# Recurrence of an RWKV-7 layer: pair group by pair group, or all eight pairs of heads chunk by chunk

## The chip, the core and the metric

The program runs on one core of a Trainium2 chip. The metric is device time in microseconds of one launch; lower is better. The core has TensorE (matmuls), VectorE, ScalarE and GpSimd, each with its own queue of instructions, and SyncE, whose queue issues nearly all DMAs. Matmuls read SBUF and write PSUM, which has eight banks of 2 KB a partition.

## The reference

The model is a trunk of two layers for a batch of 1, 1024 tokens and a width of 1024, in float32. Layer 0 mixes tokens with a Hawk block, layer 1 with RWKV-7 time mixing; each layer then has a SwiGLU block and a gated embedding. The part that the change touches is the recurrence of layer 1, over 16 heads of 64:

```python
def rwkv7_scan(r, w, k, v, a_vec, b_vec):
    def step(S, inp):
        r_t, w_t, k_t, v_t, a_t, b_t = inp
        sa = jnp.einsum('bhvk,bhk->bhv', S, a_t)
        S = S * w_t[:, :, None, :] + sa[..., None] * b_t[:, :, None, :] + v_t[..., None] * k_t[:, :, None, :]
        y = jnp.einsum('bhvk,bhk->bhv', S, r_t)
        return S, y
    S0 = jnp.zeros((B, H, N, N), jnp.float32)
    _, y = lax.scan(step, S0, xs)

def rwkv7_time_mix(x, ...):
    ...
    y = rwkv7_scan(rh, heads(decay), kh, vh, -kk, kk * ah)
    mean = jnp.mean(y, axis=-1, keepdims=True)
    var = jnp.mean(jnp.square(y - mean), axis=-1, keepdims=True)
    yn = ((y - mean) * lax.rsqrt(var + RW_GN_EPS)).reshape(B, T, D)
    yn = yn * ln_w + ln_b
    bonus = jnp.sum(rh * kh * r_k, axis=-1, keepdims=True) * vh
    out = (yn + bonus.reshape(B, T, D)) * g
    return out @ w_o, v_first
```

## The kernel before

Activations lie transposed, features on the 128 partitions, in eight tiles of 128 features, and the tokens are handled in two halves of 512 (`t` = 0 and 1). A dense float32 product is made of three fp32r matmuls of 128x128 by 512 (`mm3`, line 246): weights and activations are split into a high and a low part, and the weights are split on the fly by ScalarE and GpSimd (`load_w`, lines 238 and 239). These dense matmuls fill most of TensorE's time.

The recurrence is computed in chunks of 64 tokens, eight to a half. Two heads make a pair and lie on the two halves of the 128 partitions: `E` is partitions 0 to 63, `O` is 64 to 127, and the loops over `HV` visit both. Two pairs make a group; there are eight groups `G`, four for each half of the tokens. Four generators hold the work, written as steps that are divided by `yield`:

- `stage1` (line 990), for each pair: decays, the operands of both sides of the chunk products (`BK`, `ZL`), the scores (`sc`: for each half of the partitions four matmuls of 64 rows, 128 columns and 128 moving columns into one PSUM bank, line 1053, twice for each head), masks, and the transposed `BK` (`bkt`: eight transposes for each head, line 1079).
- `inverse` (line 1098), for each group: the inverse of a triangular 64x64 matrix for each chunk and head, by blocks.
- `stage2` (line 1176), for each group, over its eight chunks: the inputs `zu<-ZL,SV` and half of the outputs `zu<-SV,ZL` (128 rows, 64 columns), a copy `z`, the product with the inverse `zu<-z,V` (64 rows, 64 columns), copies into `SV`, the update of the state `zu<-SV,BKt` (128 rows, 64 columns), and the other half of the outputs `y<-RB,SV` (64 rows, 64 columns). Each burst handles two pairs, so four or eight matmuls. The two halves of the outputs lie in two PSUM tiles and are added by VectorE (line 1233).
- `norm2` (line 1239), for each pair: the norm over a head, the bonus and the gate (`bsum` and `yv`, one fp32 matmul of 512 columns each).

All this is fp32, and such a matmul shows as two records in the trace.

The order on TensorE is written out by hand (`manual_schedule`, line 1269). A planner keeps a clock (`mm`, line 114) that each matmul moves on by its estimated time. After each dense matmul `tick` (line 125) looks whether a generator's next step is due: each `yield` gives a wait in ns, which is multiplied by a slack (3, and 2.5 from line 1362 on), says whether a PSUM bank of the shared ring is needed, and may give a condition, such as `s2[old] >= c4 + 4` in line 1032, by which stage 1 waits until the recurrence of an earlier group has freed its buffers. If it is due, the step's matmuls are put into TensorE's queue at that place, and other engines' instructions go to theirs. `until` (line 148) puts steps into the queue, with no dense work between, until a condition holds; line 1369 does so until all generators have ended, and the tiles behind it reuse their memory. The other engines' queues are ordered by priority (`ahead`, line 107).

## Time and profile before

| what | value |
|---|---|
| median of three runs | 3106.93 us (3098.17 to 3107.34) |
| profiled execution, its own time | 3106.82 us |
| span of the profiled execution | 3105.0 us |
| mean granted TensorE clock | 0.979 |
| TensorE busy | 2958.3 us (95%), 16904 matmul records |
| VectorE busy | 1677.9 us (54%) |
| ScalarE busy | 1438.3 us (46%) |
| GpSimd busy | 1282.7 us (41%) |
| DMA | 336.04 MB, mean 108 GB/s |

The span is the time from the first to the last instruction. PE is TensorE's matmuls, PEld its weight loads, DVE VectorE, ACT ScalarE, POOL GpSimd, and SPq the queue of SyncE. A name such as `zu<-z,V` says that the tile `zu` is written from the tiles `z` and `V`. The granted clock is a share of 2.4 GHz: 1.00 is this, 0.50 is 1.2 GHz.

### The profile page before, as it was taken

What the parts mean: (1) busy time and instruction counts of PE and PEld (TensorE: products, weight loads), DVE (VectorE), ACT (ScalarE), POOL (GpSimd) and SP (SyncE); (2) the same over time, 40 slices, a digit from 0 to 9 for tenths busy, and PEclk for the clock granted to TensorE, in tenths of its full rate; (3) what the DMA queues carried; (4) which work ended last, traced back from release to release, by engine and by line L of the source; (5) the groups of instructions that cost most, each with busy time, mean ns of one, the idle gap of its engine ahead of it and who ended that gap; (6) DMA issues with size and microseconds to landing.
All of it is one profiled execution on the core that took longest, in us unless ns stands there. A gap on an engine that the chain in (4) does not pass through costs nothing. (4 is left out here: it accounts for less than half of the span.)

```text
span 3105.0 us, 45886 instructions
## 1 busy us (share of the span) xinstructions
PE 2958.3 (95%) x16904; PEld 2292.7 (74%) x16904; DVE 1677.9 (54%) x2950; ACT 1438.3 (46%) x2565; POOL 1282.7 (41%) x1080
## 2 busy tenths in 40 slices
PE   5999999999999999999998999999999999999998
PEld 3777778888776777777776667776767777888886
DVE  8756771111563266576678565777866456222145
ACT  5564752222555443444465774454344445322244
POOL 5111134444445444343434344434333355544445
PEclk9999999999998999999999999999999999999999
DMA  3211123333335464333323366423323252333323
GB/s 126 60 36 53 50 79 105 94 94 95 98 126 179 158 190 128 89 111 98 114 91 98 119 204 198 125 85 111 100 88 100 70 185 91 103 95 95 95 81 109
DMA packets 223968, 336.04 MB, mean 108 GB/s; under 512 B 56960, under 2 KB 75136, under 8 KB 223744
## 3 DMA queue, kind: packets, MB, share of 16 engines
q1 hardware_dynamic: 223456, 332.75, 34.9%
q8 instruction: 133, 2.18, 0.3%
q14 instruction: 91, 0.75, 0.1%
q10 hardware_dynamic: 288, 0.37, 0.0%
HBM read 278.24 MB, written 54.79 MB: 107 GB/s over the span
## 5 line engine op out<-in xcount | busy, mean ns | idle before, releaser
L239 POOL TENSOR_TENSOR whl<-raw,whl 128x512 fp32r<-128x512 f32 (+2 forms) x818 | 1061.8, 1303 | 1410.4 <-ACT whl L238 1319.8
L238 ACT CAST whl<-raw 128x512 fp32r<-128x512 f32 (+2 forms) x818 | 482.2, 593 | 851.5 <-PE ops L115 226.2
L115 PE MATMUL ops<-hid,whl 128*128 128x512 f32 x2112 | 523.8, 401 | 13.8 <-DVE hid L290 6.4
L115 PE MATMUL pg<-xn,whl 128*128 128x512 f32 (+1 forms) x2184 | 522.9, 392 | 4.4 <-ACT whl L238 1.9
L115 PEld LDWEIGHTS pg<-xn,whl 128*128 128x128 f32 x2184 | 405.2, 188 | 98.9 <-issue 4.3
L115 PEld LDWEIGHTS ops<-hid,whl 128*128 128x128 f32 x2112 | 392.6, 189 | 113.8 <-DVE hid L290 12.5
L115 PE MATMUL pu<-xn,whl 128*128 128x512 f32 x1584 | 385.9, 396 | 3.1 <-ACT xn L289 1.4
L115 PEld LDWEIGHTS pu<-xn,whl 128*128 128x128 f32 x1584 | 296.0, 189 | 72.0 <-DVE xn L290 2.1
L115 PE MATMUL pps<-mix,whl 128*128 128x512 f32 x1152 | 301.3, 412 | 11.9 <-ACT mix L289 5.1
L390 DVE TENSOR_TENSOR h<-h,ops 128x512 f32<-128x512 f32 x256 | 173.9, 685 | 210.6 <-PE ops L115 208.7
L555 DVE TENSOR_TENSOR sg<-sg,pu 128x512 f32<-128x512 f32 x88 | 60.4, 686 | 396.0 <-PE pu L115 395.4
L115 PEld LDWEIGHTS pps<-mix,whl 128*128 128x128 f32 x1152 | 217.7, 193 | 75.1 <-issue 7.7
L115 PE MATMUL pg<-raw,whl 128*128 128x512 f32 x720 | 198.0, 415 | 0.0
L115 PEld LDWEIGHTS pg<-raw,whl 128*128 128x128 f32 x720 | 134.4, 193 | 34.4 <-issue 3.8
L241 POOL TENSOR_SCALAR whl<-raw 128x512 fp32r<-128x512 f32 (+2 forms) x84 | 58.7, 704 | 217.6 <-PE rps L115 69.7
L115 PE MATMUL pu<-raw,whl 128*128 128x512 f32 x528 | 141.4, 406 | 0.0
L115 PE MATMUL rps<-xn,whl 128*128 128x512 f32 x480 | 123.4, 405 | 16.3 <-ACT xn L289 10.5
L115 PEld LDWEIGHTS rps<-xn,whl 128*128 128x128 f32 x480 | 91.9, 193 | 42.8 <-issue 12.0
L115 PE MATMUL gps<-xn,whl 128*128 128x512 f32 x480 | 117.9, 400 | 0.0
L115 PE MATMUL ops<-m,whl 128*128 128x512 f32 x480 | 114.4, 396 | 0.8 <-ACT m L289 0.8
L115 PEld LDWEIGHTS pu<-raw,whl 128*128 128x128 f32 x528 | 96.1, 188 | 23.8 <-issue 2.6
L115 PEld LDWEIGHTS gps<-xn,whl 128*128 128x128 f32 x480 | 92.3, 192 | 21.4 <-issue 0.5
(277 smaller groups left out, 4027.2 us busy)
## 6 DMA issues: line engine op xcount, KB each, us to landing
raw<-in_ffn_in SPq DMA_DIRECT2D x352, 256.0 KB, 2.6
raw<-in_ffn_out SPq DMA_DIRECT2D x152, 256.0 KB, 2.6
raw<-in_rkv SPq DMA_DIRECT2D x96, 256.0 KB, 3.0
raw<-in_ple_gate SPq DMA_DIRECT2D x64, 256.0 KB, 2.6
raw<-in_w_in SPq DMA_DIRECT2D x48, 256.0 KB, 2.8
h<-h SPq DMA_DIRECT2D x32, 256.0 KB, 3.5
raw<-in_ffn_out SPq DMA_DIRECT2D x48, 128.0 KB, 2.1
raw<-in_w_o SPq DMA_DIRECT2D x24, 256.0 KB, 2.7
```

The lines of the kernel that those rows point to most:

```text
L115: self.nc.tensor.matmul(out, lhsT=lhsT, rhs=rhs, start=start, stop=stop)
L238: nc.scalar.copy(hl[:rows, 0, :w], raw[:rows, :w])
L239: nc.gpsimd.tensor_sub(hl[:rows, 1, :w], raw[:rows, :w], hl[:rows, 0, :w].bitcast(F32))
L241: nc.gpsimd.tensor_scalar(hl[:rows, 0, :w], raw[:rows, :w], 1.0, 0.0, ALU.mult, ALU.add)
L390: nc.vector.tensor_add(hs, hs, ps)
L555: nc.vector.tensor_mul(sg, sg, pu)
```

## The change

- `stage2` runs once for each half of the tokens, chunk by chunk, with all eight pairs in each burst: 16 matmuls for the inputs, 16 for the inverse, 16 for the update, and 32 for the outputs. It begins when all four groups of the half are through stage 1 and the inverse. The outputs' two products go into one PSUM tile, one after the other for each pair and half of the partitions. z, the state and the outputs are handled by instructions over all eight pairs.
- Its operands go through DRAM: stage 1 writes `zl_d` (with the masked scores) and `bk_d`, the inverse writes `inv_d`, and for each chunk the recurrence loads all pairs' operands; the outputs go to `y_d`, from which the norm reads them.
- The scores of a pair's two heads alternate between the row halves, into two banks, in one burst of eight matmuls. The transposes become matmuls against a diagonal (`dg`) that holds the chunk's total decay, and these alternate in the same way, 16 in a burst.
- Stage 1 no longer waits for the recurrence. The shared ring has three PSUM banks instead of two, and a step can ask for two of them. The norm handles the two pairs of a group together.

```diff
-BANKS = 2
+BANKS = 3
...
+C0LAT, ZLAT, ULAT, SLAT = 4000, 900, 900, 3000
...
-        self.vt_d = [[self.dr.tile([64, 2, NC, 64], F32, name=f"vt{j}{t}") for t in range(2)] for j in range(KD)]
+        self.vt_d = [self.dr.tile([64, 2, NC, KD, 64], F32, name=f"vt{t}") for t in range(2)]
...
+        self.zu = pp.tile([128, KD, 64], F32, name="zu")
+        self.yp = pp.tile([128, KD, 64], F32, name="y")
...
+        self.zl_d = [self.dr.tile([128, NC, KD, 320], F32, name=f"zl{t}") for t in range(2)]
+        self.bk_d = [self.dr.tile([128, NC, KD, 128], F32, name=f"bk{t}") for t in range(2)]
+        self.inv_d = [self.dr.tile([128, NC, KD, 64], F32, name=f"inv{t}") for t in range(2)]
+        self.y_d = [self.dr.tile([128, KD, TH], F32, name=f"y{t}") for t in range(2)]
...
+                if g == jj == 0:
+                    PCs[t] = sp.tile([128, NC, KD], F32, tag="PC", name="PC", bufs=2)
+                PC = PCs[t][:, :, j]
                 nc.vector.tensor_copy(PC, Pp[:, :, 64])
-                ZL, RB = [], []
+
+                dg = sp.tile([128, NC, 64], F32, tag="dg", name="dg", bufs=1)
+                nc.gpsimd.tensor_mul(dg, ident.unsqueeze(1).to_broadcast([128, NC, 64]), PC.unsqueeze(2).to_broadcast([128, NC, 64]))
...
-                    yield 0, False, (lambda: old < 0 or s2[old] >= c4 + 4)
...
+                    zr = sp.tile([128, 4, 320], F32, tag="ZL", name="ZL", bufs=2)
+                    zl = zr[:, :, 0:256].rearrange("p c (h k) -> p h c k", h=2)
+                    rb = zr[:, :, 256:320]
...
-                    yield 1500, True, None
-                    for hh, me, ot in HV:
-                        ps = big("sc", 1700).rearrange("p (c s) -> p c s", c=4)
-                        for c in range(4):
-                            self.mm(ps[:, c, :], BK[me, c4 + c, :, :].rearrange("p i s -> p (i s)"), zl[me, hh, c, :])
-                        evac()
-                        m3 = mask.unsqueeze(1).to_broadcast([128, 4, 128])
-                        with self.ahead(AHEAD_S1):
+                    yield 1500, 2, None
+
+                    pss = [big("sc", e).rearrange("p (c s) -> p c s", c=4) for e in (1000, 2000)]
+                    for c in range(4):
+                        for hh, me, ot in HV:
+                            self.mm(pss[hh][:, c, :], BK[me, c4 + c, :, :].rearrange("p i s -> p (i s)"), zl[me, hh, c, :])
+                            if hh:
+                                self.clock -= 200
+                    evac()
+                    evac()
+                    m3 = mask.unsqueeze(1).to_broadcast([128, 4, 128])
+                    with self.ahead(AHEAD_S1):
+                        for hh, me, ot in HV:
+                            ps = pss[hh]
                             nc.vector.tensor_mul(AB[me, cs, :], ps[me, :, 0:64], m3[me, :, 0:64])
                             nc.vector.tensor_mul(rb[me], ps[me, :, 64:128], m3[me, :, 64:128])
                             nc.vector.tensor_mul(zl[ot, hh], ps[ot], m3[ot])
-                        if hh == 0:
-                            yield 0, True, None
-                yield 0, True, (lambda: (G == 0 or inv[G - 1] >= 1) and (old < 0 or s2[old] == NC))
+                    nc.sync.dma_start(self.zl_d[t][:, cs, j, :], zr)
+                yield 0, 2, (lambda: (G == 0 or inv[G - 1] >= 1))
...
-                for hh, me, ot in HV:
-                    ps = c3(big("bkt", 800))
-                    for c in range(NC):
-                        nc.tensor.transpose(ps[:, c, :], BK[me, c, :, :].rearrange("p i s -> p (i s)"), ident[me])
...
+                pss = [c3(big("bkt", e)) for e in (500, 900)]
+                for c in range(NC):
+                    for hh, me, ot in HV:
+                        self.mm(pss[hh][:, c, :], BK[me, c, :, :].rearrange("p i s -> p (i s)"), dg[me, c, :])
+                        self.clock -= 77
+                evac()
+                evac()
+                with self.ahead(AHEAD_S1):
+                    for hh in range(2):
+                        nc.scalar.copy(BKt[:, :, hh, :], pss[hh])
+                nc.sync.dma_start(self.bk_d[t][:, :, j, :], BKt.rearrange("p c h k -> p c (h k)"))
...
-                yield 0, False, (lambda: G == 0 or s2[G - 1] == NC)
...
+                nc.sync.dma_start(self.inv_d[G // 4][:, :, 2 * (G % 4) : 2 * (G % 4) + 2, :], Vt)
...
         def stage2():
             ahead = lambda: self.ahead(AHEAD_S2)
+            def state():
+                return sp.tile([128, 2, KD, 64], F32, tag="SV", name="SV", bufs=2)
+            def load(t, c, SV):
+                ZL = sp.tile([128, KD, 320], F32, tag="ZC", name="ZC", bufs=2)
+                V = sp.tile([128, KD, 64], F32, tag="VC", name="VC", bufs=2)
+                for hh, me, ot in HV:
+                    nc.sync.dma_start(SV[ot, hh], self.vt_d[t][:, hh, c])
+                nc.sync.dma_start(ZL, self.zl_d[t][:, c])
+                nc.sync.dma_start(V, self.inv_d[t][:, c])
+                return ZL, V, SV
+            def load_u(t, c):
+                SU = sp.tile([128, 2, KD, 64], F32, tag="SU", name="SU", bufs=1)
+                BKc = sp.tile([128, KD, 128], F32, tag="BC", name="BC", bufs=1)
+                for hh, me, ot in HV:
+                    nc.sync.dma_start(SU[ot, hh], self.vt_d[t][:, hh, c])
+                nc.sync.dma_start(BKc, self.bk_d[t][:, c])
+                return SU, BKc
+            SV = state()
+            for hh, me, ot in HV:
+                nc.gpsimd.memset(SV[me, hh], 0.0)
+            for t in range(2):
+                yield 0, False, (lambda: inv[4 * t + 3] == 3 and s1[4 * t + 3] == 22 and all(have("v", j, t)() for j in range(KD)))
+                PC = PCs[t]
+                nxt = load(t, 0, SV)
+                yield C0LAT, False, None
                 for c in range(NC):
+                    ZL, V, SV = nxt
+                    SU, BKc = load_u(t, c)
                     upd = not (t == 1 and c == NC - 1)
+                    ps, yp = self.zu, self.yp
+                    z = sp.tile([128, KD, 64], F32, tag="z", name="z", bufs=1)
+                    at = self.clock
+                    for j in range(KD):
                         for hh, me, ot in HV:
+                            self.mm(ps[me, j, :], ZL[:, j, hh * 128 : hh * 128 + 64], SV[:, hh, j, :])
+                    self.clock = at + 650
+                    with ahead():
+                        nc.scalar.copy(z, ps)
+                        if upd:
+                            ss = sp.tile([128, KD, 64], F32, tag="ss", name="ss", bufs=1)
+                            for hh, me, ot in HV:
+                                nc.vector.tensor_mul(ss[me], SV[me, hh], PC[me, c, :].unsqueeze(2).to_broadcast([64, KD, 64]))
+                            SVn = state()
+                        if c < NC - 1:
+                            nxt = load(t, c + 1, SVn)
+                    yield ZLAT, False, None
+                    at = self.clock
+                    for j in range(KD):
                         for hh, me, ot in HV:
+                            self.mm(ps[me, j, :], V[me, j, :], z[me, j, :])
+                    self.clock = at + 600
+                    with ahead():
+                        nc.scalar.copy(SU[E, 0], ps[E])
+                        nc.vector.tensor_copy(SU[O, 1], ps[O])
+                    yield ULAT, False, None
+                    at = self.clock
+                    if upd:
+                        for j in range(KD):
+                            for hh, me, ot in HV:
+                                self.mm(ps[me, j, :], BKc[:, j, hh * 64 : hh * 64 + 64], SU[:, hh, j, :])
                         with ahead():
+                            for hh, me, ot in HV:
+                                nc.vector.tensor_add(SVn[me, hh], ps[me], ss[me])
+                    for j in range(KD):
                         for hh, me, ot in HV:
+                            self.mm(yp[me, j, :], SV[:, hh, j, :], ZL[:, j, hh * 128 + 64 : hh * 128 + 128], True, False)
+                            self.mm(yp[me, j, :], SU[me, hh, j, :], ZL[me, j, 256:320], False, True)
+                    self.clock = at + 2000
+                    if c % 2 == 0:
+                        ys = sp.tile([128, KD, 2, 64], F32, tag="yc", name="yc", bufs=1)
+                    with ahead():
+                        nc.scalar.copy(ys[:, :, c % 2, :], yp)
+                    if c % 2:
+                        nc.sync.dma_start(self.y_d[t][:, :, c * 64 - 64 : c * 64 + 64], ys.rearrange("p j c k -> p j (c k)"))
                     if upd:
+                        SV = SVn
+                    s2[t] = c + 1
+                    yield SLAT, False, None
...
         def norm2():
...
+                yield Y1, 2, None
...
+                yield 2400, 2, None
...
```

## Rows read from the trace of the kernel before

**Rows 1.** The page's engine line: busy us, share of the span, instructions.
```profile
PE 2958.3 (95%) x16904; PEld 2292.7 (74%) x16904; DVE 1677.9 (54%) x2950; ACT 1438.3 (46%) x2565; POOL 1282.7 (41%) x1080
```
**Rows 2.** Windows: stretch, its length, busy us (records) by engine, clock, DMA share, GB/s.
```profile
500.00:800.00 300.00, 298.29 (x1292) 241.96 (x1292) 65.85 (x81) 90.50 (x150) 140.00 (x108) 1.00 0.31 94
1125.00:1715.00 590.00, 565.53 (x4178) 430.16 (x4177) 399.82 (x837) 274.24 (x554) 249.64 (x206) 0.98 0.37 109
1950.00:2530.00 580.00, 558.05 (x4527) 420.44 (x4527) 388.07 (x839) 254.73 (x537) 232.16 (x179) 0.98 0.35 103
```
**Rows 3.** TensorE's timeline, one chunk step: start, length, operation, tiles, records.
```profile
1277.99 0.34 PE L115 MATMUL zu<-SV,ZL 128*64 128x64 f32 x4
...
1278.61 1.88 PE L115 MATMUL ops<-hid,whl 128*128 128x512 f32 x7
1280.42 0.45 PE L115 MATMUL zu<-z,V 64*64 64x64 f32 x8
1280.80 2.34 PE L115 MATMUL ops<-hid,whl 128*128 128x512 f32 x9
1283.07 0.45 PE L115 MATMUL zu<-SV,BKt 128*64 128x64 f32 x8
1283.45 0.45 PE L115 MATMUL y<-RB,SV 64*64 64x64 f32 x8
1283.83 2.59 PE L115 MATMUL ops<-hid,whl 128*128 128x512 f32 x10
1286.34 0.34 PE L115 MATMUL zu<-SV,ZL 128*64 128x64 f32 x4
```
**Rows 4.** TensorE's timeline at a burst of scores.
```profile
1238.04 1.16 PE L115 MATMUL sc<-ZL,BK 64*128 64x128 f32 x8
1239.13 1.66 PE L115 MATMUL pu<-xn,whl 128*128 128x512 f32 x6
1240.72 1.16 PE L115 MATMUL sc<-ZL,BK 64*128 64x128 f32 x8
```
**Rows 5.** TensorE's timeline at a burst of transposes.
```profile
1264.73 0.70 PE L1079 MATMUL bkt<-cst,BK 64*128 64x64 f32 x8
1265.36 3.00 PE L115 MATMUL ops<-hid,whl 128*128 128x512 f32 x12
```
**Rows 6.** The tile of the scores: records, ns min/median/max, first and last start.
```profile
L115 PE MATMUL sc<-ZL,BK x512: 271/272/580, 1132.4 to 2358.8; 64*128 64x128 f32 x171
```
**Rows 7.** TensorE's timeline at the lora matmuls (128 and 64 rows in turn).
```profile
955.45 4.24 PE L115 MATMUL lx<-lora,whl 128*128 128x512 f32 x10
...
965.98 13.06 PE L115 MATMUL lx<-lora,whl 128*128 128x512 f32 x18 [3.61 <-DVE y L766]
```
**Rows 8.** Windows around them and at a short stretch of lower clock.
```profile
955.40:961.30 5.90, 5.42 (x14) 2.22 (x13) 4.03 (x7) 2.74 (x4) 4.15 (x4) 1.00 0.51 162
961.30:981.80 20.50, 16.89 (x27) 7.69 (x27) 7.28 (x10) 17.29 (x31) 8.09 (x7) 0.50 0.59 218
1582.50:1585.90 3.40, 3.40 (x9) 2.73 (x9) 2.04 (x6) 1.48 (x5) 0.00 (x0) 0.50 0.30 77
```
**Rows 9.** Groups of ScalarE: count, busy us, mean ns, idle before, releasers.
```profile
L1203 ACT ACTIVATE ss<-SV,PC 64x64 f32<-64x64 f32 x240 | 82.8, 345 | 51.5 <-DVE SV L1220 41.4 <-DMA SV<-st 4.7 <-DMA st<-ss 1.6
```
**Rows 10.** Waits of TensorE, 1125 to 2530 us: total, times, longest us.
```profile
PE zu L115 <- DVE z L1199: 4.7, 4, 2.0
```
**Rows 11.** Waits of SyncE's queue in the same stretch.
```profile
SPq L227 <- POOL whl L239: 834.9, 332, 10.4
```
**Rows 12.** TensorE's timeline at the end of the scan.
```profile
2503.51 1.02 PE L115 MATMUL yv<-v,cst 128*128 128x512 f32 x2
...
2524.32 5.76 PE L115 MATMUL pg<-raw,whl 128*128 128x512 f32 x24
```

More of the change, by code (lines that the diff above doesn't have):

```diff
@@ L122, in ready @@
         lat, bank, cond = st.need
-        return (cond is None or cond()) and max(lat, self.bank_free[self.bank_n % BANKS] if bank else 0.0)
+        return (cond is None or cond()) and max([lat] + [self.bank_free[(self.bank_n + i) % BANKS] for i in range(int(bank))])
     def tick(self, wait=False):
@@ L959, in t3 @@
         def t3(nm):
-            return sp.tile([128, TH], F32, tag="t3", name=nm, bufs=2)
+            return sp.tile([128, TH], F32, tag="t3", name=nm, bufs=4)
         def ld(nm, j, t, tt=tt):
@@ L1170, in inverse @@
                     for p0 in (0, 64):
[L1171 to L1172 removed]
+                        nc.scalar.copy(V[p0 : p0 + 32, :, :, 32:64], ps[p0 : p0 + 32].rearrange("p (j c) k -> p j c k", j=2))
+                nc.sync.dma_start(self.inv_d[G // 4][:, :, 2 * (G % 4) : 2 * (G % 4) + 2, :], Vt)
                 yield 1000, False, None
@@ L1177, in stage2 @@
             ahead = lambda: self.ahead(AHEAD_S2)
-            for G in range(NG):
-                t, g = G // 4, G % 4
-                pairs = 2 * g, 2 * g + 1
-                yield 0, False, (lambda: inv[G] == 3 and s1[G] == 22 and (G == 0 or n2[G - 1]))
-                ys = [sp.tile([128, TH], F32, tag="ys", name="ys", bufs=2) for j in pairs]
+            def state():
[8 more added lines that the diff above has]
+                return ZL, V, SV
@@ L1222, in stage2 @@
-                    for ps, ZL, RB, z, ss, PC, BKt, SV, V, yp in T:
-                        for hh, me, ot in HV:
-                            self.mm(yp[me, cc, :], SV[me, c, hh, :], RB[me, cc, :])
-                    if upd and c == NC - 1:
-                        for j, x in zip(pairs, T):
-                            nc.sync.dma_start(self.st_d[j], x[4])
-                    if cc == 3:
-                        with ahead():
-                            for jj in range(2):
-                                y = ys[jj][:, (c - 3) * 64 : (c + 1) * 64].rearrange("p (c s) -> p c s", s=64)
-                                nc.scalar.copy(y, yps[:, jj])
-                                nc.vector.tensor_add(y, y, self.zu[jj][:, 3:7])
```

112 lines of the change are left out of this document (30 added, 82 removed).

## The prediction

> **What bounds the kernel now.** The page's engine line comes first: TensorE is busy 95% of the span, no other engine over 54% [rows 1]. So the time is the sum of what is queued on TensorE, plus its waits, plus what a lower clock costs. The windows tell the dense part from the part with the recurrence [rows 2]. From 500 to 800 us there is dense work alone: 1292 matmuls in 298.29 us, 0.231 us each. From 1125 to 1715 and from 1950 to 2530 us the recurrence lies between the dense matmuls; TensorE is idle 24.5 and 22 us there, VectorE is busy 68 and 67%, and the clock is 0.98. An instruction of the recurrence that TensorE no longer runs is therefore saved almost whole, and one that lasts longer there is paid almost whole. VectorE and ScalarE count only where TensorE waits for them.
>
> The timeline of one chunk step is the next view [rows 3]: from 1277.99 to 1286.34 us, 8.35 us, it holds 7 + 9 + 10 = 26 dense matmuls, 6.01 us at 0.231. The recurrence of one pair group and chunk thus costs 2.34 us. There are 64 such steps (8 groups, 8 chunks): 150 us. An fp32 matmul shows as two records. The first burst (8 matmuls, 16 records, one tile shape) reaches the next dense matmul after 0.62 us, the second (4 matmuls) after 0.38 us. Four more matmuls cost 0.24 us, 0.06 each, the two column halves side by side; 0.14 us is left that does not depend on their number. The same 0.38 us stands between the start of the update (128x64) and that of the outputs (64x64), with no dense work and no wait between: a change of tile shape costs 0.14 us there too. The dense runs behind the bursts are longer than their count (7 in 1.81 us instead of 1.62, 9 in 2.27 instead of 2.08, 10 in 2.51 instead of 2.31): 0.20 us more. A burst costs 0.34 us, and 0.06 per matmul.
>
> **The change part by part.** The sum is made against the profiled execution, 3106.82 us (span 3105.0 and 1.8 around it); the median of the runs, 3106.93, is the same.
>
> *Fewer bursts.* Three bursts in each of 64 steps, 192, become three in each of 16 chunks, 48. Inputs (16 matmuls), inverse (16) and update (16) now cost 0.34 + 16 x 0.06 = 1.30 us each, 3.9 us a chunk.
>
> *The outputs of a chunk.* Both products go into one PSUM tile, so for each pair and half the code issues one matmul with 128 rows and then one with 64 rows: 32 in a row whose tile shape changes every time. Before, each kind stood in a group of four. One alone between two changes costs 0.14 us and its own time, from 0.06 us (as beside its partner) to 0.12 (alone): 0.20 to 0.26. The nearest row of such a stream is the lora one, which also changes between 128 and 64 rows each time [rows 7]: 10 matmuls in 4.24 us, 0.42 instead of 0.231, so 0.19 more for each change, which gives 0.06 + 0.19 = 0.25. I take 0.26: 32 x 0.26 = 8.3 us. A chunk then costs 3.9 + 8.3 = 12.2 us, 16 chunks 195 us, against 150 now: **+45 us**. With 0.20 it is 10.3 and 165 us (+15); if the change of shape were free, 32 x 0.06 = 1.9, so 5.8 and 93 us (-57).
>
> This is where the Trainium skill speaks against the change. "TensorEngine Tiling (Array Packing)", Key Properties, says that changing the tiling mode, not only the tile, drains the engine. The trace agrees: 0.14 us at each change [rows 3]. The page gives no duration; read as a drain of the whole array it makes the +45, read tile by tile it makes the first rival.
>
> *The scores.* A burst of four takes 1.09 us to the next dense matmul, and the six dense ones behind it 1.59 instead of 1.39 [rows 4]: 1.29 us. There are 64 (512 records, [rows 6]): 82 us. After, 32 bursts hold eight each, alternating between the row halves in two banks. One matmul with no partner is (1.09 - 0.14)/4 = 0.24 us. Side by side the burst stays at 1.29 us: 41 us in all, **-41**. One after the other it is 0.34 + 8 x 0.24 = 2.24: 72 us, -11. No row shows two row halves at once; the nearest, the column halves of rows 3, do overlap fully, so I take -41.
>
> *The transposes.* A burst of eight takes 0.63 and 0.20 us [rows 5]; 32 make 27 us. They become 16 bursts of 16 fp32 matmuls against a diagonal, their stationary side the same 128 columns as the scores'. At 0.12 each (row halves side by side) a burst is 2.26 us, 36 in all: **+9**. Serial at 0.24 it is 4.2 us: +40. At 0.06, since only 64 columns move: -6. I take +9, as the stationary side equals the scores'.
>
> *The clock.* The lora stream again: 5.9 us after its first matmul, with 0.5 us idle in it, the granted clock falls to 0.50, and it stays there while 18 alternating matmuls run for 13.06 us without a gap, 0.73 each instead of 0.42, 1.7 times as long [rows 7, 8]. The outputs last 8.3 us. If the clock falls 5.9 us into them, the last 2.4 us cost 1.7 more. Then dense work begins at the lower level; the shortest such stretch here is 3.4 us with nine dense matmuls where 14.7 would fit [rows 8], 1.3 us lost. 16 x 3.0 = **+48 us**. Bounds: 0 if it never falls; 90 if it falls halfway and two such stretches follow (16 x (3.0 + 2.6)).
>
> *VectorE, ScalarE.* The small evacuations go: ScalarE's scaling of the state alone is 240 instructions, 82.8 us [rows 9]; 8 wide ones per chunk replace them. Neither engine sets the time, so I cost this at nothing. The waits it could end are few: 4.7 us for z [rows 10]. But stage 1 no longer waits for the recurrence, so its VectorE work moves closer together: VectorE's 400 us in 590 hold four groups and about 130 us of dense work (0.22 of the time [rows 2]), so some 270, under 60 per group without recurrence and output norm. By the waits in the code a group now comes every 70 us or so, with 15 of dense work: VectorE is full there, and TensorE may wait 5 us a group, 40 in all. The other way, half of the 46 us idle could go. I take nothing, from -25 to +40.
>
> *The transfers.* Each chunk now fetches 2.6 MB and stage 1 writes as much, about 80 MB more. All is issued on SP's queue, where weight loads already wait 834.9 us for their buffers, up to 10.4 us at once [rows 11]; behind such a wait stand the new loads. The next chunk's operands are asked for a chunk ahead, over 20 us. The update's come at the start of their own chunk, some 7 us ahead: if one is 4 us late each time, 64 us; I take nothing, since the issue may run ahead of TensorE.
>
> *The end.* The second half's recurrence starts only when all its groups are through stage 1. The last work of the scan stands at 2503.51 us, the dense work that must not start before it at 2524.32 [rows 12]: 21 us of cover. After, from the waits in the code: the first scores still near 1880 us, as r is ready no earlier; a pair's waits are 1 + 4 + 1.5 + 1.5 = 8 us times a slack of 3, with bursts and banks some 36 us, so eight pairs end near 2170; the inverse takes 45; a chunk waits 0.9 + 0.9 + 3 = 4.8 us times 2.5, with its 12.2 some 25, eight of them 200; an output norm waits 7.4 us times 2.5, some 22, four of them 88. That is near 2505, while the dense work moves out with the sum. So nothing; were the waits to be half again as long for the pairs, as waits for banks and VectorE could make them, the end lies some 65 us past the cover.
>
> **Sum**: 3107 + 45 - 41 + 9 + 48 = 3168 us.
>
> **The rivals.**
> 1. *Faster: the changes of shape cost little.* The outputs write one column half after the other; if one half drains while the other runs, a matmul costs 0.13: a chunk 3.9 + 4.2 = 8.1, 130 in all, -20; with -41 and +9 and no fall of the clock, 3055 us. If they are free, -57: 3018. For it: the column halves run side by side in rows 3. Against: the 0.14 us stands at each change there. Without the clock it decides at (150 + 32)/16 = 11.4 us a chunk, less 3.9: 7.5, 0.23 us per output matmul; below that the kernel is faster.
> 2. *The row halves don't overlap*: scores -11 and transposes +40, 61 us more: 3229. For it: no row shows the overlap. Against: the column halves.
> 3. *Late data*: operands behind weight loads (+64), or the scan past its cover (+65): about 3233.
> 4. *The change gives back what it takes*: the clock holds and half of the idle goes: 3107 + 13 - 15 = 3105.
>
> **How the numbers follow.** Forecast 0.48, with its own range from 3091 (0.20 each, clock holds) to 3215 (clock term 90). Rival 1 0.24, rival 2 0.12, rival 3 0.10, rival 4 0.06. About 0.3% (9 us) can be told from no change. Faster: rival 1, 0.03 of the forecast's low end, 0.01 of rival 4: 0.28. Same: 0.03 of the forecast and 0.04 of rival 4: 0.07. Slower: 0.65. The range: rival 1's freer half (0.11) stays out below 3045; rivals 2 and 3 go in up to 3260, which leaves 0.08 above.
>
> **What would show it.** The outputs' run of 64 records per chunk: 8 us long or longer if I am right, 2 us if the changes of shape are free. The score bursts: 1.1 us for 16 records, or 2. The clock row: a fall in most chunks between the first and last of them, or none. Idle of TensorE before the update names a late load; idle before the last output norms, the end. The forecast is wrong if the outputs take under 7 us and the clock stays at 1.00.

## The result and the profile after

The changed kernel takes 3224.57 us (median of four runs, 3217.91 to 3224.96) where the kernel before takes 3102.55 beside it: a ratio of 1.039 [1.036, 1.042], slower. The forecast was 3168 us in a range of 3045 to 3260. The direction and the place of the loss hold. The size does not: +61 us were forecast, and the profiled executions differ by 118 (spans 3222.9 and 3105.0). The measured time also lies above 3215, the upper end of the forecast's own range; it falls into the stated range through the part up to 3260, which was put there for rivals 2 and 3.

The page's engine line of the changed kernel, against [rows 1], shows TensorE 80 us busier although it has nearly the same number of records; VectorE and ScalarE are 60 and 79 us less busy.

```profile
PE 3038.5 (94%) x17160; PEld 2386.2 (74%) x17160; DVE 1618.0 (50%) x2498; ACT 1359.2 (42%) x2213; POOL 1301.1 (40%) x1082
```

The windows, against [rows 2] (the second stretch with the recurrence now ends some 110 us later), show dense work alone unchanged and a clock of 0.94 and 0.89 where it was 0.98.

```profile
500.00:800.00 300.00, 298.29 (x1292) 241.98 (x1291) 65.74 (x80) 90.89 (x150) 139.10 (x108) 1.00 0.31 94
1125.00:1715.00 590.00, 565.08 (x4525) 448.54 (x4524) 338.99 (x614) 222.25 (x383) 226.96 (x180) 0.94 0.50 159
1990.00:2640.00 650.00, 604.89 (x4610) 474.67 (x4608) 338.89 (x594) 215.74 (x366) 227.22 (x178) 0.89 0.46 147
```

TensorE's timeline of one chunk, against [rows 3]. The first three bursts are short: 32 records in 1.08 (1523.50 to 1524.58), 1.08 and 0.98 us. The outputs then run for 9.43 us, a new tile shape every two records: each lone matmul takes 0.26 us (1533.19 to 1533.45), and 0.40 at the end, where the clock has fallen.

```profile
1523.50 1.15 PE L116 MATMUL zu<-SV,ZC 128*64 128x64 f32 x32
1524.58 2.79 PE L116 MATMUL pu<-xn,whl 128*128 128x512 f32 x11
...
1527.75 1.15 PE L116 MATMUL zu<-z,VC 64*64 64x64 f32 x32
1528.83 3.25 PE L116 MATMUL pg<-xn,whl 128*128 128x512 f32 x13
1532.00 1.15 PE L116 MATMUL zu<-SU,BC 128*64 128x64 f32 x32
1532.98 0.28 PE L116 MATMUL y<-ZC,SV 128*64 128x64 f32 x2
1533.19 0.33 PE L116 MATMUL y<-ZC,SU 64*64 64x64 f32 x2
1533.45 0.33 PE L116 MATMUL y<-ZC,SV 128*64 128x64 f32 x2
...
1540.80 0.47 PE L116 MATMUL y<-ZC,SV 128*64 128x64 f32 x2
1541.20 0.47 PE L116 MATMUL y<-ZC,SU 64*64 64x64 f32 x2
...
1542.41 3.88 PE L116 MATMUL pg<-xn,whl 128*128 128x512 f32 x9
```

Windows over the outputs' runs alone (the first, the last, and the sum of all 16) give 155.8 us for them; the clock is below 1.00 in each, 0.64 to 0.87.

```profile
1532.98:1542.41 9.43, 9.43 (x64) 6.82 (x64) 0.00 (x0) 0.00 (x0) 0.00 (x0) 0.82 0.29 86
...
2518.80:2529.89 11.09, 11.09 (x64) 7.94 (x64) 0.00 (x0) 0.00 (x0) 0.00 (x0) 0.64 0.10 25
sum 155.79, PE 155.77 PEld 112.55 DVE 0.68 ACT 0.00 POOL 2.72; mean PE 9.74 PEld 7.03 DVE 0.04 ACT 0.00 POOL 0.17
```

The same windows stretched to 20 us from each run's start hold the dense work behind it as well. Eleven of the 16 read 0.83, four 0.74 and the last 0.66, as in these two; which makes 20 x (11 x 0.17 + 4 x 0.26 + 0.34) x 2 = 130 us at 0.50, 69 of them in the runs and 61 in the dense work behind.

```profile
1532.98:1552.98 20.00, 20.00 (x110) 15.43 (x107) 4.12 (x6) 4.65 (x8) 3.48 (x4) 0.83 0.45 142
...
2518.80:2538.80 20.00, 20.00 (x92) 15.03 (x92) 2.07 (x3) 3.64 (x7) 3.10 (x3) 0.66 0.24 76
```

**A split that serves every run.** I split each span into three: idle time of TensorE (before and between its matmuls), the price of the clock (half of the time that TensorE is busy at 0.50), and the rest, the work at full clock. Before, these are 139, 60 and 2906 us. They are summed over the trace's records; span x (1 - mean clock), which also counts idle time at 0.50, gives 65 for before and 161 instead of 145 for after. The differences against before, in us of the profiled executions:

| kernel | ratio to before | span | work | clock | idle | work by the prediction's terms |
|---|---|---|---|---|---|---|
| the change | 1.039 [1.036, 1.042] | +118 | -4 | +85 | +38 | +13 |
| e1 outputs grouped | 0.996 [0.995, 0.997] | -13 | -88 | +23 | +52 | -89 |
| e2 half the changes of shape | 1.005 [1.004, 1.007] | +13 | -55 | +21 | +46 | -52 |
| e3 outputs in four pieces | 1.047 [1.045, 1.049] | +139 | +16 | +48 | +75 | +29 |
| e4 scores in turn | 1.044 [1.042, 1.045] | +134 | +15 | +81 | +38 | +34 to +49 |
| f3 the scores alone | 1.003 [1.002, 1.004] | +10 | -35 | +15 | +30 | -41 |
| f4 alternating outputs alone | 1.055 [1.052, 1.058] | +174 | +91 | +37 | +45 | +93 |
| n1 before, other order | 1.015 [1.013, 1.017] | +51 | +2 | +19 | +31 | 0 |
| n2 two banks, in turn | 1.002 [1.001, 1.003] | +2 | -17 | -9 | +29 | -11 |
| f1 e1, slower stage 1 | 0.997 [0.996, 0.998] | -20 | -86 | +12 | +53 | -89 |
| f2 e1, operands stored twice | 1.003 [1.002, 1.004] | +2 | -85 | +17 | +70 | -89 |
| f5 e1, norm loads on ScalarE's queue | 1.003 [1.002, 1.005] | +6 | -88 | +25 | +68 | -89 |
| f6 e1, longer bank estimates | 0.998 [0.997, 1.000] | -5 | -83 | +30 | +48 | -89 |

Span, work, clock and idle of a row are of one execution, the ratio of all. For n1 it is the slowest of four (3157.66 us, median 3147.06) and for f1 the fastest of ten (3086.39, median 3094.41), so by the medians n1 is 43 us above the kernel before, not 51, and f1 9 below, not 20.

Two things stand out. In ten of the thirteen the work is within 6 us of the terms. The others are the change, e4 and e3. The change and e4 hold the long alternating runs, and there the split is some 10 us off: at 0.50 an alternating matmul lasts 0.40 us instead of 0.256, 1.57 times as long, not twice, so the half is too much for the 69 us in the runs. The change's own split is then +6 of work and +75 of clock. In e4 the price of the scores was too high as well (below); e3's 13 us less than the terms are not explained. And every kernel that differs from the kernel before has at least 29 us more idle time, n1 too, in which no part of the change is made.

### The profile page after: what moved, and what is told of

Read it like the earlier page. It is cut to its first block, busy times and chain, and to the rows that moved or that the text cites. A ratio compares the mean times of both kernels' runs of the same rounds, so it can differ in the third digit from the quotient of the medians.

```text
span 3222.9 us, 45692 instructions
## 1 busy us (share of the span) xinstructions
PE 3038.5 (94%) x17160; PEld 2386.2 (74%) x17160; DVE 1618.0 (50%) x2498; ACT 1359.2 (42%) x2213; POOL 1301.1 (40%) x1082
## 5 line engine op out<-in xcount | busy, mean ns | idle before, releaser
L116 PE MATMUL ops<-hid,whl 128*128 128x512 f32 x2112 | 513.1, 400 | 19.0 <-ACT hid L290 7.2
L116 PEld LDWEIGHTS ops<-hid,whl 128*128 128x128 f32 x2112 | 400.8, 192 | 119.6 <-DVE hid L291 14.3
L116 PE MATMUL pps<-mix,whl 128*128 128x512 f32 x1152 | 297.6, 412 | 15.2 <-ACT mix L290 4.6
L116 PEld LDWEIGHTS pg<-raw,whl 128*128 128x128 f32 x720 | 145.9, 206 | 39.6 <-ACT whl L239 3.0
L116 PEld LDWEIGHTS pu<-raw,whl 128*128 128x128 f32 x528 | 105.7, 203 | 28.4 <-ACT whl L239 2.2
L291 DVE TENSOR_TENSOR hid<-sg,hid 128x512 fp32r<-128x512 f32 x88 | 86.3, 980 | 49.8 <-ACT hid L290 49.7
```

Source lines behind the costliest of these rows:

```text
L116: self.nc.tensor.matmul(out, lhsT=lhsT, rhs=rhs, start=start, stop=stop)
L291: (nc.gpsimd if pool else nc.vector).tensor_sub(lo, src, hi.bitcast(F32))
```

## The experiments on the outputs

**e1.** All 128-row products of a chunk, then all 64-row ones: one change of shape instead of 32 between the outputs. Each half of the partitions becomes one accumulation group, started once. By the Trainium skill, "PSUM — Partial Sum Buffer", section "The four PSUM rules", a start clears the written marks of the whole bank on all the partition quarters that it writes, so that with a second start the later products would overwrite the first ones instead of being added to them; no run here shows that.

```diff
                     for j in range(KD):
                         for hh, me, ot in HV:
-                            self.mm(yp[me, j, :], SV[:, hh, j, :], ..., True, False)
-                            self.mm(yp[me, j, :], SU[me, hh, j, :], ZL[me, j, 256:320], False, True)
+                            self.mm(yp[me, j, :], SV[:, hh, j, :], ..., j == 0, False)
+                    for j in range(KD):
+                        for hh, me, ot in HV:
+                            self.mm(yp[me, j, :], SU[me, hh, j, :], ZL[me, j, 256:320], False, j == KD - 1)
```

> All 16 output products of 128 rows of a chunk, then all 16 of 64 rows: one change of tile shape instead of 32. Theory (each change costs about 0.14 us and the overlap of the halves, and the long run of changes lowers the clock): a chunk's output run shrinks from 9 to 11 us to about 2.1 (32 x 0.06 + 0.14), 16 x 7.4 = 118 us, the falls of the clock in it go, some 30 us more of dense work at the lower level: 3070 to 3090 us, below the kernel before. Rival (VectorE's lateness in stage 1 and the chunk's loads set the time): within 20 us of the changed kernel, 3205 to 3225.

3093.67 us: 131 us faster than the change, and 0.4% faster than the kernel before; 4 us past the upper end of what was expected. VectorE's and GpSimd's instructions stand in the same order as in the change. The tile's records in e1 (ns min/median/max of one) are as short as in any burst, a chunk's outputs take 2.11 us, and no fall of the clock begins at them:

```profile
L116 PE MATMUL y<-ZC,SV x512: 222/222/270, 1534.0 to 2399.2; 128*64 128x64 f32 x171
L116 PE MATMUL y<-ZC,SU x512: 218/218/267, 1535.0 to 2400.3; 64*64 64x64 f32 x171
```

**e2.** Both heads' 128-row products, then both 64-row ones: 16 pairs instead of 32 lone matmuls.

```diff
                         for hh, me, ot in HV:
                             self.mm(yp[me, j, :], SV[:, hh, j, :], ..., True, False)
+                        for hh, me, ot in HV:
                             self.mm(yp[me, j, :], SU[me, hh, j, :], ZL[me, j, 256:320], False, True)
```

> For each pair both halves' 128-row products, then both 64-row ones: 16 changes of shape a chunk instead of 32, and the halves beside each other. Theory: 2 x 0.14 + 4 x 0.06 = 0.52 us a pair, 4.2 us a chunk instead of 9 to 11, 16 x 5.4 = 86 us; falls of the clock become rare: 3110 to 3140 us. Rival (the cost goes with the number of matmuls, not of changes): no difference, 3215 to 3230.

3120.82 us, as expected. A pair, one head on each column half, takes 0.26 us, as one matmul alone does in the change; a chunk 4.17 us, without a fall. So the price belongs to the change of shape, not to the matmul.

```profile
1534.01 0.29 PE L116 MATMUL y<-ZC,SV 128*64 128x64 f32 x4
1534.22 0.33 PE L116 MATMUL y<-ZC,SU 64*64 64x64 f32 x4
...
1538.17 2.12 PE L116 MATMUL pg<-xn,whl 128*128 128x512 f32 x8
```

**e3.** The same 32 alternating matmuls in four pieces, dense work between them.

```diff
                     for j in range(KD):
+                        if j in (2, 4, 6):
+                            self.clock = at + 600
+                            yield 700, False, None
+                            at = self.clock
...
-                    self.clock = at + 2000
+                    self.clock = at + 600
...
-                    yield SLAT, False, None
+                    yield SLAT - 2100, False, None
```

> The same 32 changes of shape a chunk, but in four pieces with about 2 us of dense work between. Theory with the clock: no piece is long enough for the clock to fall; a piece takes 8 x 0.26 = 2.1 us, three more bursts cost 3 x 0.34 = 1.0 us a chunk (+16), and the 16 falls of 6.8 to 13.7 us go (-50 to -80): 3160 to 3195 us, no fall of the clock at the outputs. Rival (the clock costs nothing here, only the changes of shape): 3230 to 3245.

A piece takes 2.05 us, as expected, and only two falls begin at one. The time is a miss: 3246.14 us. That is next to the rival's band, but not for the rival's reason, as the clock's price fell from +85 to +48 us. The pieces removed most of the outputs' clock price, and the idle time went from +38 to +75. The waits of TensorE in e3 from 1125 to 2700 us (total, times, longest) show loads for which the changed kernel waits 0.5 us in all. The shortened wait in front of the next chunk is the likely reason; no run separates it from the pieces.

```profile
PE zu L116 <- DMA SU<-vt: 14.9, 12, 1.9
PE bsum L116 <- DMA b<-b: 14.8, 4, 6.9
```

**f4.** The kernel before with the outputs' eight matmuls of each step alternating in the last burst. The 128-row products stand behind the write of the solution there and read it in place of the state, so what they compute is another; their number and shapes are the same.

```diff
-                        for hh, me, ot in HV:
-                            self.mm(ps[me, 3 + cc, :], SV[:, c, hh, :], ZL[:, hh, cc, 64:128])
...
                         for hh, me, ot in HV:
+                            self.mm(ps[me, 3 + cc, :], SV[:, c, hh, :], ZL[:, hh, cc, 64:128])
                             self.mm(yp[me, cc, :], SV[me, c, hh, :], RB[me, cc, :])
```

> The kernel before with the other part alone: in each of the 64 chunk steps the four matmuls of 128 rows of the outputs move from the first burst to the last one, where they alternate with the four of 64 rows; 8 matmuls in a row whose tile shape changes each time, some 2 us. Theory A (each lone matmul between two changes of shape costs 0.26 us, whether the clock falls or not): 8 x 0.26 = 2.1 us for the eight, against 8 x 0.06 plus the one change 0.14 = 0.62 that they cost before: +1.46 x 64 = +93 us, near 3197, ratio 1.025 to 1.033, with the granted clock staying up at nearly all of the 64 runs, as they end before 3 us. Theory B (what the changes cost in the changed kernel is mainly the lower clock that follows a long run of them): without a fall of the clock the time rises by 40 us or less, ratio 1.013 or below.

The work is +91 us, and A's +93 holds. But the time is +174, a ratio of 1.055, which neither theory expected. The new place has a wait of its own, of which A took no account (waits of TensorE from 1150 to 2560 us: 33.8 us in 49), and the clock price grew by 37 us: 17 falls begin at or just behind these runs. Runs of 2 us, here with a wait of some 0.6 us in front of each, do not keep the clock up as I expected.

```profile
PE zu L115 <- DVE SV L1218: 33.8, 49, 1.8
```

## The experiments on the scores and the waits

**e4.** The scores of the changed kernel one head after the other, still two banks at once.

```diff
-                    for c in range(4):
-                        for hh, me, ot in HV:
+                    for hh, me, ot in HV:
+                        for c in range(4):
                             self.mm(pss[hh][:, c, :], BK[me, c4 + c, :, :]..., zl[me, hh, c, :])
```

> The scores of one head after those of the other in the same burst, so that neighbouring matmuls lie on the same row half. Theory (row halves run side by side in the changed kernel): the burst of 16 records goes from 0.9 to 1.8 us, 32 x 0.9 = +29 us: 3245 to 3260. Rival (the gain of the score bursts is only their number): 3220 to 3230.

3240.25 us, 16 us slower than the change and between the two bands. In turn a burst lasts 1.64 us to the next dense matmul, where the prediction's price is 2.04 (2.24 less the 0.20 in the dense work behind). Alternating the heads is thus worth 0.55 us a burst, 32 x 0.55 = 18 us, near the 19 by which the work grew. The timeline of e4, and behind it that of the changed kernel, 1.09 us:

```profile
1131.99 1.71 PE L116 MATMUL sc<-ZL,BK 64*128 64x128 f32 x16
1133.63 3.71 PE L116 MATMUL pps<-mix,whl 128*128 128x512 f32 x15
```

```profile
1132.79 1.16 PE L116 MATMUL sc<-ZL,BK 64*128 64x128 f32 x16
1133.88 1.89 PE L116 MATMUL pps<-mix,whl 128*128 128x512 f32 x7
```

**f3.** The kernel before with the row-half scores alone.

```diff
-                    yield 1500, True, None
-                    for hh, me, ot in HV:
-                        ps = big("sc", 1700)...
-                        for c in range(4):
-                            self.mm(ps[:, c, :], BK[me, c4 + c, :, :]..., zl[me, hh, c, :])
+                    yield 1500, 2, None
+                    pss = [big("sc", e)... for e in (1000, 2000)]
+                    for c in range(4):
+                        for hh, me, ot in HV:
+                            self.mm(pss[hh][:, c, :], BK[me, c4 + c, :, :]..., zl[me, hh, c, :])
+                            if hh:
+                                self.clock -= 200
...
```

> The kernel before with one part of the change alone: the scores of the two heads of a pair are issued in turn on the two row halves, into two PSUM banks, in bursts of 16 records; all else stays (chunk steps by pair groups, transposes, outputs in groups of one shape). Theory A (the two halves run side by side, and the saving reaches the end, as my sum has it): a burst of eight lasts about 0.9 us to the next dense matmul, 64 bursts become 32, and the time falls by about 41 us: near 3064, ratio 0.986 to 0.990. Theory B (side by side, but the burst that now needs two banks at once waits for their evacuation, in the middle of the burst, with the lower clock after each such wait): the records stand in pairs as in A, but waits of TensorE of the kind scores on the evacuation of the bank come to 10 us or more, and the time falls by 15 us or less: ratio 0.995 or above.

Most of the 41 us is there (work -35), and none of it arrives: idle +30, clock +15. B's ratio is met (1.003), yet its mechanism is not the one: the waits of the scores for a bank are 5.6 us, and the large ones stand in the norm of the outputs (TensorE's waits from 1150 to 2560 us: total, times, longest).

```profile
PE bsum L115 <- issue: 15.2, 3, 10.1
PE bsum L115 <- DMA b<-b: 10.0, 1, 10.0
...
PE sc L115 <- DVE ZL L1065: 5.6, 4, 2.8
```

**n2.** f3 with the heads in turn (the loops of e4), so that the joint burst and its two banks are new; the planner's clock also counts each matmul in full, without f3's `-= 200`.

> The kernel before with both heads' scores in one burst that needs two banks, as in the change, but one head after the other, not side by side. Work: one fixed cost of 0.34 us less in each of 32 bursts, so -11 us against before. Theory B (the need of two banks at once makes the waits): idle 20 to 35 us more and the clock 5 to 20, as with the scores side by side: ratio 1.004 to 1.014. Theory C (the waits come because side by side the burst ends sooner and its results come faster than VectorE clears them): idle and clock within 10 us of before, ratio 0.993 to 1.000.

Idle +29, as in f3, though the two heads' results now come one after the other: C falls. B's idle time is there, but its clock price is not (-9), and the ratio, 1.002, lies between the bands of the two. The work is -17 where -11 was expected, since a burst in turn is shorter than its price, as in e4.

**n1.** The kernel before with a single estimate changed.

```diff
-                    yield 1500, True, None
+                    yield 2500, True, None
```

> The kernel before, with no part of the change: only the wait that the order by estimates puts before each scores burst is 2500 instead of 1500 ns, so the same instructions stand in another order on TensorE. I split each span into idle time of TensorE, what the lower clock costs (half of the time that TensorE is busy at it) and the rest, its work: the scores alone on the row halves took 35 us of work away and gave back 30 of idle and 15 of clock. Theory A (the order of the kernel before fits its waits closely, and any other order pays for it, whatever was made faster): work within 6 us of before, idle and clock together 20 to 45 us more, ratio 1.006 to 1.014. Theory B (the waits come from what the scores burst newly needs, two banks at once): idle and clock within 10 us, ratio 0.997 to 1.003.

1.0145 [1.0125, 1.0165]: A, a little past the upper end of what A expected. The work is the same within 2 us, idle +31, clock +19, together past the 45 as well, though in the slowest of its four executions. Up to 1715 us it is idle hardly more than the kernel before (26 instead of 24.5 us from 1125 on); 25 of the 31 us stand behind 1950 us. No burst has grown and no second bank is asked for. The longest waits of TensorE from 1125 to 2700 us, of the kernel before, of n1 and of the changed kernel:

```profile
PE bsum L115 <- issue: 8.9, 2, 6.2
PE yv L115 <- ACT v L1252: 5.7, 4, 3.0
```

```profile
PE sc L115 <- DVE ZL L1059: 13.6, 3, 7.2
PE ops L115 <- DVE h L390: 11.4, 5, 5.4
PE nps L115 <- DVE acc L301: 9.6, 4, 4.6
```

```profile
PE sc L116 <- DVE ZL L1072: 16.8, 4, 6.1
PE nps L116 <- DVE acc L302: 9.3, 2, 5.8
PE lx L116 <- DVE o L896: 7.4, 1, 7.4
```

**f6, f5, f1, f2** start from e1 and each take one candidate for its 52 us. f6 sets longer bank estimates, f5 moves the norm's loads from SP's queue to ScalarE's, f1 slows stage 1 in the first half, f2 stores the scores' operands twice.

```diff
-                    pss = [big("sc", e)... for e in (1000, 2000)]
+                    pss = [big("sc", e)... for e in (2500, 3500)]
```

> e1 (outputs grouped by shape), with larger estimates for the evacuation of the two banks of a scores burst (2500 and 3500 ns instead of 1000 and 2000), so that the next burst is set later in the order of TensorE and dense work is put before it. Theory A (a good part of the idle time of TensorE is the scores waiting in the middle of a burst for their second bank): the waits of the scores on VectorE's evacuation fall below 4 us from 10 or more, the idle time of 1158 to 2512 us falls from 112 to under 100 and the time falls by 10 to 20 us: ratio to the kernel before 0.990 to 0.993. Theory B (those waits are only where a delay of VectorE shows first): they move to other lines (inverse, transposes, lora) with the same sum, and the ratio stays within 0.003 of e1's 0.9964.

The scores' waits halve (15.2 to 7.5 us), but the idle time of 1158 to 2512 us goes from 115 to 108 only, the clock gets worse, and the ratio rises to 0.9984 [0.9970, 0.9998]: the waits moved, for example to `ops` (10.5 us at once, behind ScalarE's `on`). A falls. B's ratio is met (0.0020 above e1's), though the waits went to other lines than it named: summed over 1125 to 2700 us, those that end on VectorE fall from 71 to 29 us, and those that end on ScalarE, GpSimd and loads rise from 50 to 87.

```diff
-                    nc.sync.dma_start(ys, self.y_d[t][:, j, :])
+                    nc.scalar.dma_start(ys, self.y_d[t][:, j, :])
...
```

> The changed kernel with its outputs grouped by shape (e1), and in addition the loads of the output norms (y, b, v, g) issued on ScalarE's queue instead of SP's. Theory A (the part of the time that my sum lacks is waits behind SP's queue: the norms' loads and stores stand there in order with those of the dense work): TensorE's idle time between 1707 and 1950 us falls from 39.7 us to 20 or less, and the time falls by 15 to 25 us from e1: ratio to the kernel before 0.988 to 0.992. Theory B (those waits come from the shared transfer engines, or from VectorE's and ScalarE's own order): the idle time stays above 32 us, and the ratio stays between 0.994 and 1.000, or goes up, as ScalarE then stands behind its own loads.

1.003: A falls. Idle of 1707 to 1950 us goes up from 40 to 45 us, and the loads that I moved are now late themselves (waits of TensorE, 1150 to 2560 us):

```profile
PE bsum L116 <- DMA b<-b: 29.3, 6, 10.7
```

```diff
-                yield 4000, False, (lambda: old < 0 or inv[old] >= 2)
+                yield 4000 + 3000 * (t == 0), False, (lambda: old < 0 or inv[old] >= 2)
```

> e1 (the changed kernel with its outputs grouped by shape), with 7000 instead of 4000 ns of waiting between two pairs of heads of stage 1 in the first half. Theory D (stage 1 without its wait on the recurrence runs at the pace of VectorE, and TensorE waits for that): of the 24 us idle and 27 us at the lower clock between 1158 and 1544 us 10 or more of each go, and the ratio to before is 0.990 to 0.994. Rival (any order of this kernel has such waits, they move): idle and clock together within 10 us of e1 or more, ratio 0.995 to 1.000.

Idle of 1158 to 1544 us is 23 us (24 in e1), and the time at the lower clock there falls from 27 to 17 us; but over 1158 to 2512 us the time at the lower clock is the same 126 us, and the ratio lies within e1's interval: the rival. The pace of stage 1 in the first half is not what makes TensorE idle there. The second half was not slowed.

```diff
                     nc.sync.dma_start(self.zl_d[t][:, cs, j, :], zr)
+                    nc.sync.dma_start(self.zl2_d[t][:, cs, j, :], zr)
```

> e1 with each store of the scores' operands (640 KB, 32 times) issued a second time to another place in DRAM: 21 MB more. Theory E (the 80 MB of operands that go through DRAM make part of the waits, by SP's order or by the shared transfer engines): with a quarter more of them idle and clock grow by 10 us or more, ratio 1.000 or above. Rival (the transfers are covered, as my sum has it): within 8 us of e1, ratio 0.994 to 0.999.

1.0033 [1.0022, 1.0044], idle +18 against e1. E's number is met, but not cleanly: TensorE's waits for loads from 1125 to 2700 us are 0.5 us in all (4.8 in e1), so it does not wait for late loads itself; and TensorE's order is the same as e1's, while those of VectorE, ScalarE and SP shift with the 32 added issues, and n1 shows what another order alone can do.

## Why the prediction was right in sign and half in size

- **Fewer bursts and the outputs: right.** 0.26 us for each lone matmul, 32 x 0.26 = 8.3 us a chunk; at full clock the trace has 0.256 (32 in 8.2). e2 and f4 price the same change of shape, and e1 takes it away: 2.11 us, near the 1.9 that I gave to outputs without the changes. The 0.26 measured lies above the point of decision, 0.23 us per matmul, so rival 1 is out.
- **The scores and transposes: right in work.** Records stand in pairs 7 ns apart, so rival 2 is out; f3's -35 stands beside my -41. A burst of transposes takes 1.93 us (2218.49 to 2220.42 in the timeline below) where I had 2.06, beside the 0.20 in the dense work behind. The price of the other end was too high: e4's 1.64 us instead of 2.04. The work is +6 instead of +13; the transposes and the 8.2 us of the outputs make 4 of these 7.
- **The clock at the outputs: right, 55 instead of 48.** It falls in all 16 runs, 3.2 to 6.6 us after their start (I had 5.9), and stays down for 6.8 to 13.7 us. The runs are 155.8 - 16 x 8.2 = 25 us longer for it (I had 27), and the 61 us of dense work at 0.50 lose 30 (I had 21).
- **Late loads and the end: right at nothing, the end partly by luck.** No load of the chunk's operands is among TensorE's waits. The last `yv` stands at 2626.41, 121 us behind the 2505 that I had; `ops`, which may run beside it, lasts until 2639. The `pu` and `pg` behind it start at 2639.05 and 2642.48, the latter held up by a weight for 2.59 us, so the dense work moved out by 118 us and the scan by 123 (TensorE's timeline):

```profile
2626.41 1.88 PE L116 MATMUL yv<-v,cst 128*128 128x512 f32 x4
2627.72 11.49 PE L116 MATMUL ops<-hid,whl 128*128 128x512 f32 x48
2639.05 0.84 PE L116 MATMUL pu<-raw,whl 128*128 128x512 f32 x3
2642.48 0.73 PE L116 MATMUL pg<-raw,whl 128*128 128x512 f32 x2 [2.59 <-ACT whl L239]
```

- **The range: held by luck.** 3224.57 us lies above the forecast's own upper end of 3215. The room up to 3260 was there for rivals 2 and 3, and neither came true. Two slips had no effect: half of the 46 us idle in rival 4 is 23 us, not 15, which gives 3097; and the upper end with a clock term of 90 is 3210, not 3215.
- **"VectorE, ScalarE: I take nothing" is the step that failed.** Idle rose by 38 us, within the +40 at which I ended the range of this term but not at its middle value. Away from the outputs the clock took 20 more (75 less 55), which no term of the sum had: 58 us together. The parts add up: -7 of work, +7 of clock at the outputs and +58 of waits are the gap between 61 and 118. The +40 was put on VectorE being full in stage 1, and that reason was nearer than the zero. On the mean VectorE is not full: in the later part of the second half's stage 1, where TensorE is idle for 34 us, it is busy for 214 of 310 us, 69% (windows of the changed kernel).

```profile
2010.00:2320.00 310.00, 275.94 (x2580) 221.57 (x2580) 214.29 (x416) 113.73 (x196) 126.42 (x101) 0.91 0.47 148
```

  But the waits end on it. Summed over 1125 to 2700 us TensorE waits 107 us instead of 71, and 34 of these 36 us more end on VectorE (63 instead of 29). In the 19 of them that last 0.8 us or more (59 us) VectorE is busy for 84% of the time, which points to work that has piled up there and not to its mean load. f1 says little on this. It slowed the first half, and the idle time grew in the second: from 1125 to 1715 us it is 24.9 us (24.5 before), from 1990 to 2640 us 45 (22 from 1950 to 2530 before). So what costs is single waits of up to 7 us, at places that differ from kernel to kernel, and the clock after them. Outside the outputs' runs each of the 22 falls of the clock between 1125 and 2700 us comes shortly behind a wait of 0.8 us or more; the 16 at the outputs come without one.

One such wait in the changed kernel, in TensorE's timeline and in VectorE's. The burst of scores starts with 2 of its 16 records; the other 14 wait 6.13 us for the second bank, since VectorE's evacuations of the burst before (`AB<-sc`, `ZL<-sc`) stand behind `PC<-Pp`, which waits for ScalarE, and behind 2.40 us of work for the state `ss`. VectorE was busy for 10.76 of the 11 us up to 2201. The window after the wait reads a clock of 0.69, and the 14 records take 1.97 us.

```profile
2200.51 0.48 PE L116 MATMUL sc<-ZL,BK 64*128 64x128 f32 x2
2207.14 2.04 PE L116 MATMUL sc<-ZL,BK 64*128 64x128 f32 x14 [6.13 <-DVE ZL L1072]
2209.11 0.79 PE L116 MATMUL ops<-hid,whl 128*128 128x512 f32 x1
...
2218.49 2.00 PE L116 MATMUL bkt<-dg,BK 64*128 64x64 f32 x32
2220.42 1.88 PE L116 MATMUL pu<-raw,whl 128*128 128x512 f32 x7
```

```profile
2202.28 0.81 DVE L1031 COPY PC<-Pp 128x8 f32<-128x8 f32 x1 [0.97 <-ACT Pp L1006]
2203.12 2.40 DVE L1229 TENSOR_TENSOR ss<-SV,PC 64x512 f32<-64x512 f32 x2
2205.53 0.42 DVE L1070 TENSOR_TENSOR AB<-sc,cst 64x256 f32<-64x256 f32 x1
...
2206.30 0.69 DVE L1072 TENSOR_TENSOR ZL<-sc,cst 64x512 f32<-64x512 f32 x1
```

```profile
2190.00:2201.00 11.00, 11.00 (x59) 8.49 (x57) 10.76 (x29) 2.23 (x5) 2.70 (x3) 1.00 0.35 121
...
2207.00:2214.00 7.00, 6.87 (x31) 5.75 (x32) 6.67 (x15) 1.14 (x2) 1.51 (x2) 0.69 0.61 190
```

**Shown:** another order of unchanged instructions costs this kernel +31 us of idle and +19 of clock (n1; +43 in all by the medians), nearly as much as the change has of both beside its outputs (38 and 20). The order before leaves few such waits, and all thirteen kernels that moved its bursts have more of them, so a term of zero for the waits was no middle value here. That every other order would cost as much is not shown: n1 is a single one, which sets the scores later.

**Open:** how much of the change's 38 us comes from the order alone, how much from bursts that need two banks (n2 cannot tell the two apart, f6 moved the waits without ending them) and how much from the bytes (f2 is mixed with an order). Part of it may also be that TensorE gets ahead of the others (an argument, not shown): from the change to e1, with VectorE's and GpSimd's order unchanged, TensorE has 84 us less work and 14 us more idle time. VectorE's load in the second half's stage 1 was not tested by a run. An order fitted anew to e1 was not tried; if it had the idle time and the clock of before, e1's work of -88 us would all arrive, near 3020 us. That is an estimate from the split, and no run has shown it.

## What to carry to other kernels

Put matmuls of one tile shape together, across all the heads of a burst if need be: here the order of two loops was worth 131 us (3224.57 to 3093.67). Where TensorE is 95% busy under a written-out order, price a change in three sums, work, clock and waits, and give the waits of a new order a value above zero: here 13 changed kernels had 29 to 75 us more idle time. An engine that is busy for half of the span can still be full where a burst waits for it, so its mean load does not give this value. Test it with the shift of one estimate, which changes no instruction, before a gain in work is counted on.

## What the runs showed of the hardware that I had not expected

Scores issued in turn still overlap in part: in e4 a second stream of records begins 6 ns after the fifth record of a burst, while three of the first head's are still to come, which makes the 1.64 us. Two heads side by side, 16 records, last as long as one head's 8: 1.09 us both [rows 4]. A change of shape costs the same 0.26 us to the next change whether one matmul lies between, or two on the two column halves. And in f4 the clock fell in 17 of 64 steps with 2 us of alternating matmuls and waits of about 0.6 us between dense work, in e3 at 2 of its 64 pieces of the same length: what sets it off in the one and not in the other stays open.
